# Time mixing of an RWKV-7 layer: small products of even and odd chunks laid on all four quarters of the matmul array

## The chip, the cores and the metric

The kernel runs on one core of one Trainium2 chip. The metric is the device time of one execution in microseconds. The engines are PE (TensorE: matmuls, with PEld for its weight loads), DVE (VectorE), ACT (ScalarE), POOL (GpSimd) and SP (SyncE, which issues the loads). Each takes its instructions in the order in which the program gives them; semaphores tie the engines together. A matmul contracts over partitions (rows of the array) and writes to partitions of PSUM (columns of the array). PSUM has eight banks of 2 KB for each partition; a bank holds 512 float32.

## The reference, cut to what matters

Two layers on 256 positions with 2048 features. The change touches the first, an RWKV-7 time mixing with 32 heads of 64 features:

```
def step(S, inp):
    r_t, w_t, k_t, v_t, kk_t, a_t = inp
    sa = einsum('bhvk,bhk->bhv', S, -kk_t)
    S = S * w_t[:, :, None, :] + sa[..., None] * (kk_t * a_t)[:, :, None, :] + v_t[..., None] * k_t[:, :, None, :]
    y = einsum('bhvk,bhk->bhv', S, r_t)
    return S, y
```

y is then normalised in each head, a bonus is added, and the result is gated and multiplied by `w_o`. The rest is a shared K/V, a chunked attention layer and two MLPs; they take most of the time and are not touched.

## The kernel before

**Pairs and chunks.** The recurrence is computed in four chunks of 64 positions. Two heads form a pair: their 2 x 64 features fill the 128 partitions, and there are 16 pairs. A feature-major tensor has features on partitions and positions in columns (`k`, `r`, `v`, `kr`, `bh`, `kh`). A time-major one has, for each chunk, the 64 positions on partitions: head 0's copy on partitions 0 to 63, head 1's on 64 to 127 (`vp`, `mk`, `ar`, `bk`, `da`, `co`, `u`). Nearly all of a pair's products are 64x64 or 64x128 in float32, one for each head; the head is the slice `K` of partitions on both sides. So they use two quarters of the array: rows and columns 0 to 63 for head 0, rows and columns 64 to 127 for head 1. A float32 product is two matmul instructions in the trace.

**Steps and slots.** A pair runs through 36 steps (`yield`): 8 early, 12 of inversion, 16 late. A new pair begins every 8 slots, so four or five are alive at once. In a slot each living pair issues one step (inversions first), then 1/8 of a pair's dense work: the projections `k` and `r` (`proj_steps`, 16 x 3 full matmuls each, four slots each). In three of four slots one step of an unrelated matrix-vector product follows (`ada`: a 512 KB load of `w_ada` into a `raw` buffer, then `acc` on DVE, L460). When the projections are done, 36 slots of a drain follow in which the dense work is the start of the output projection (`out_steps`). A scheduler sets each engine's order; the slots steer it.

**The steps that matter here:**

- `vp` (early step 7): `each` (L105) multiplies each chunk of `v` by `cen`; output in `ms`, copied by ACT (L186).
- First inversion step: `each` makes `bh` times `kr` for four chunks, 64x128 each, into `gr`; DVE masks it to `ar` (L217), six small ACT copies take `da` and `co` (L223, L225); POOL makes `u` and `al` from them.
- Second inversion step: two `each` with `eye` transpose two tensors into `ms`; ACT copies them to `bk` (L237).
- Further inversion steps: 32x32 products (L111) into `iv`, at the last level into `ms`; at level 2, `each` makes `kh` times `kr` into `gr`, and DVE masks it to `mk` (L267). DVE's transpose `tt` (L243) and ACT's copy `xs` lie between them.
- Late, for each chunk c three steps. First: `mk` times `vp` (L284, the value product) and `kr` times the state `zs` (L287), copied to `g`. Second: `u` times `g` (L291), negated to `sa`. Third: three products into y (L295, L298, L300) and two into the new state (L304, L306), which DVE adds to `zs` (L309, L311).

**PSUM in this stage.** `ms` two banks, `pj` two (the projections alternate), `gr`, `iv` one each, `lt` two (one for each of the two pairs that are late at once). ACT copies a finished projection out of `pj` (L870). Weights come as 512 KB loads into six `raw` buffers (L372); ACT rounds them to `wH` (L382), DVE takes the rest to `wL` (L385).

Of the kernel before, what the change touches and what calls it, by code (L numbers as in the profile page):

```python
# [77 lines left out]
class Pair:  # L78
# [23 lines left out]
    def each(self, o, lhsT, rhs):  # L102
        for c in range(4):
            for K in self.heads:
                self.b.nc.tensor.matmul(o(c)[K], lhsT(c)[K], rhs(c)[K], start=True, stop=True)  # L105
# [22 lines left out]
    def early(self):  # L128
# [55 lines left out]
        pt = b.psm().rearrange("p (a c k) -> p a c k", a=2, c=4)  # L184
        self.each(lambda c: pt[:, 0, c, :], lambda c: ch(v)[:, c, :], lambda c: cst("cen"))
        nc.scalar.copy(self.vp, pt[:, 0])  # L186
# [6 lines left out]
    def corner(self, l):  # L193
        t = self.b.psm() if l == 5 else self.b.pp.tile([P, 512], F32, tag="iv", bufs=1, name="iv")
        return t.rearrange("p (c t) -> p c t", t=H)[:, 0:4, :]

    def invert(self):
# [10 lines left out]
        ui = cst("ui").unsqueeze(1).to_broadcast([P, 4, P])  # L208
# [5 lines left out]
        pg = pp.tile([P, 4, P], F32, tag="gr", bufs=1, name="gr")  # L214
        self.each(lambda c: pg[:, c, :], lambda c: ch(bh)[:, c, :], lambda c: kr[:, c, :])
        ar = self.ar = s("ar", 3)
        nc.vector.tensor_tensor(out=ch(ar), in0=pg[:, :, C:P], in1=ui[:, :, C:P], op=ALU.mult)  # L217
# [3 lines left out]
        for i, K in enumerate(QS):  # L221
            n = H * (i % 2)
            nc.scalar.copy(da[K], pg[K, :, n:n + H])  # L223
            if i % 2 == 0:
                nc.scalar.mul(co[K], pg[K, :, H:C], -1.0)  # L225
# [7 lines left out]
        pt = b.psm().rearrange("p (a c k) -> p a c k", a=2, c=4)  # L233
        for i, t in enumerate(ts):
            self.each(lambda c: pt[:, i, c, :], lambda c: ch(t)[:, c, :], lambda c: cst("eye"))
        bk = self.bk = b.pw.tile([P, 2, 4, C], F32, tag="bk", bufs=3, name="bk")
        nc.scalar.copy(bk, pt)  # L237
# [3 lines left out]
        for l in range(1, 6):  # L241
# [21 lines left out]
            if l == 2:  # L263
                pg = pp.tile([P, 4, P], F32, tag="gr", bufs=1, name="gr")
                self.each(lambda c: pg[:, c, :], lambda c: ch(kh)[:, c, :], lambda c: kr[:, c, :])
                mk = self.mk = self.big("mk", 3)
                nc.vector.tensor_tensor(out=mk, in0=pg, in1=ui, op=ALU.mult)  # L267
            yield

    def late(self):  # L270
        b, nc, j, s, ch, v = self.b, self.b.nc, self.j, self.s, self.ch, self.v
        kr, ar, mk, bk, vp, u, pc, heads = self.kr, self.ar, self.mk, self.bk, self.vp, self.u, self.pc, self.heads
# [3 lines left out]
        pch, py = bank[:, 0, 0:3 * C].rearrange("p (a t) -> p a t", a=3), bank[:, 1, :]  # L276
        zs = None
        for c in range(4):
# [4 lines left out]
            for K in heads:  # L283
# [958 lines left out]
```

## Time and profile before

| | before |
|---|---|
| median of 3 runs | 2656.92 us (2656.05 to 2656.99) |
| span of the profiled execution | 2653.8 us |
| mean granted PE clock | 0.993 |
| PE busy | 2574.9 us, 97% |
| DVE busy | 2089.4 us, 79% |
| ACT busy | 1368.6 us, 52% |
| time mixing with pairs | about 217 to 690 us |

The page has one profiled execution. The median of the runs lies 3.1 us above its span; no time is given for that execution beside the span. A row of a timeline is: start in us, duration in us, engine, line, operation, output<-inputs, shapes, number of instructions; in square brackets the idle time of the engine just before and who ended it. Matmuls overlap in the pipeline, so the time that one takes on PE is read from one start to the next and not from its duration. Rows of a stretch give, for each of PE, PEld, DVE, ACT and POOL, the busy us and the number of instructions, then the granted clock, the DMA share and GB/s. The chain is the chain of work that ended last, followed back.

### The profile page before, as it was taken

What the parts mean: (1) busy time and instruction counts of PE and PEld (TensorE: products, weight loads), DVE (VectorE), ACT (ScalarE), POOL (GpSimd) and SP (SyncE); (2) the same over time, 40 slices, a digit from 0 to 9 for tenths busy, and PEclk for the clock granted to TensorE, in tenths of its full rate; (3) what the DMA queues carried; (4) which work ended last, traced back from release to release, by engine and by line L of the source; (5) the groups of instructions that cost most, each with busy time, mean ns of one, the idle gap of its engine ahead of it and who ended that gap; (6) DMA issues with size and microseconds to landing.
All of it is one profiled execution on the core that took longest, in us unless ns stands there. A gap on an engine that the chain in (4) does not pass through costs nothing.

```text
span 2653.8 us, 59231 instructions
## 1 busy us (share of the span) xinstructions
PE 2574.9 (97%) x24108; PEld 2257.3 (85%) x24108; DVE 2089.4 (79%) x3054; ACT 1368.6 (52%) x2484; POOL 210.6 (8%) x338
## 2 busy tenths in 40 slices
PE   7999999999999999999999999999999999999997
PEld 4788888887899888888888998887898888888886
DVE  6888878878789888888888898899887556555555
ACT  3346555555456445355365554565564464453554
POOL 1002223223110000000001000000100000000002
PEclk9999999999999999999999999999999999999999
DMA  9976656565768888989888779887766555555553
GB/s 351 320 243 220 211 181 196 180 197 196 253 234 301 325 320 320 329 325 334 325 328 293 237 247 326 313 282 263 266 216 236 191 186 188 190 187 188 189 189 121
DMA packets 207664, 663.19 MB, mean 250 GB/s; under 512 B 21408, under 2 KB 55072, under 8 KB 207392
## 3 DMA queue, kind: packets, MB, share of 16 engines
q1 hardware_dynamic: 205328, 656.89, 71.7%
q8 instruction: 189, 3.10, 0.5%
q10 hardware_dynamic: 2064, 2.53, 0.3%
q14 instruction: 83, 0.68, 0.1%
HBM read 657.23 MB, written 2.10 MB: 248 GB/s over the span
## 4 chain that ended last, share of the span: by engine, by line
PE 84%; DVE 7%; issue 4%; DMA 3%; ACT 2%; POOL 1%; SPq 0%; DVEq 0%; ACTq 0%; POOLq 0%
PE pj L416 42%; PE pj L418 21%; PE pj L405 3%; PE pj L406 3%; PE pj L407 3%; DMA raw<-w_ada 2%; DVE wL L385 2%; DVE acc L460 1%; PE iv L111 1%; PE o L405 1%; PE ms L328 1%; PE o L407 0%; ACT wH L382 0%; PE o L406 0%; PE pT L1130 0%
## 5 line engine op out<-in xcount | busy, mean ns | idle before, releaser
L385 DVE TENSOR_TENSOR wL<-raw,wH 128x1024 fp32r<-128x1024 f32 x772 | 941.1, 1220 | 342.4 <-ACT wH L382 337.2
L382 ACT CAST wH<-raw 128x1024 fp32r<-128x1024 f32 x772 | 806.0, 1045 | 762.7 <-PE pj L416 590.2
L416 PE MATMUL pj<-aHL,wH 128*128 128x512 f32 x2816 | 893.3, 398 | 1.1 <-DVE x L955 1.1
L416 PE MATMUL pj<-hHL,wH 128*128 128x512 f32 x2048 | 644.7, 396 | 0.0
L418 PEld LDWEIGHTS pj<-aHL,wL 128*128 128x128 f32 x2816 | 531.7, 189 | 123.1 <-issue 0.3
L418 PE MATMUL pj<-aHL,wL 128*128 128x256 f32 x2816 | 564.1, 281 | 0.0
L418 PEld LDWEIGHTS pj<-hHL,wL 128*128 128x128 f32 x2048 | 384.5, 188 | 91.1 <-DVE wL L385 0.9
L416 PEld LDWEIGHTS pj<-aHL,wH 128*128 128x128 f32 x2816 | 432.1, 189 | 8.6 <-issue 8.3
L418 PE MATMUL pj<-hHL,wL 128*128 128x256 f32 x2048 | 402.6, 278 | 0.4 <-DVE wL L385 0.4
L460 DVE SCALAR_TENSOR_TENSOR acc<-rada,ct,acc 128x1024 f32<-128x1024 f32 x256 | 327.3, 1278 | 7.3 <-DMA rada<-w_ada 6.9
L416 PEld LDWEIGHTS pj<-hHL,wH 128*128 128x128 f32 x2048 | 312.2, 189 | 1.3 <-DVE hHL L1001 1.1
L405 PE MATMUL pj<-aHL,wH 128*128 128x256 f32 (+1 forms) x896 | 262.5, 293 | 0.0
L406 PE MATMUL pj<-aHL,wH 128*128 128x256 f32 (+1 forms) x896 | 254.2, 284 | 0.0
L407 PE MATMUL pj<-aHL,wL 128*128 128x256 f32 (+1 forms) x896 | 253.0, 282 | 0.0
L524 POOL TENSOR_TENSOR ss<-ss,sq 128x256 f32<-128x256 f32 x56 | 51.2, 915 | 1583.7 <-ACT sq L523 1583.4
L1026 DVE SCALAR_TENSOR_TENSOR x<-pj,mod,x 128x256 f32<-128x256 f32 x256 | 123.3, 482 | 64.2 <-PE pj L418 61.2
L405 PEld LDWEIGHTS pj<-aHL,wH 128*128 128x128 f32 x896 | 169.9, 190 | 4.5 <-issue 0.2
L407 PEld LDWEIGHTS pj<-aHL,wL 128*128 128x128 f32 x896 | 170.4, 190 | 0.4 <-DVE e L851 0.2
L406 PEld LDWEIGHTS pj<-aHL,wH 128*128 128x128 f32 x896 | 169.9, 190 | 0.5
L460 DVE SCALAR_TENSOR_TENSOR acc<-raw,ct,acc 128x1024 f32<-128x1024 f32 x104 | 138.0, 1327 | 17.4 <-DMA raw<-w_ada 17.2
L998 ACT ACTIVATE t<-t 128x256 f32<-128x256 f32 x112 | 46.9, 419 | 120.2 <-DVE t L970 120.2
L1001 DVE TENSOR_TENSOR hHL<-t,hHL 128x256 fp32r<-128x256 f32 x128 | 53.9, 421 | 1.7 <-ACT t L1000 1.0
(252 smaller groups left out, 2817.6 us busy)
## 6 DMA issues: line engine op xcount, KB each, us to landing
raw<-w_up SPq DMA_DIRECT2D x256, 512.0 KB, 4.0
raw<-w_down SPq DMA_DIRECT2D x256, 512.0 KB, 3.6
rada<-w_ada SPq DMA_DIRECT2D x209, 512.0 KB, 5.5
raw<-w_ada SPq DMA_DIRECT2D x111, 512.0 KB, 4.3
rada<-w_ada_kv SPq DMA_DIRECT2D x64, 512.0 KB, 6.6
rawa<-w_ada SPq DMA_DIRECT2D x32, 512.0 KB, 6.7
rawa<-w_ada_t SPq DMA_DIRECT2D x32, 512.0 KB, 7.1
raw<-w_k SPq DMA_DIRECT2D x32, 512.0 KB, 3.6
```

The costliest lines, as they stand in the source:

```text
L382: nc.scalar.copy(Hf, raw)
L385: eng.tensor_tensor(out=Lf, in0=raw, in1=Hf, op=ALU.subtract)
L405: nc.tensor.matmul(ps, H[:, i, :], a(kt)[:, 0, :], start=(first and kt == 0), stop=False)
L406: nc.tensor.matmul(ps, H[:, i, :], a(kt)[:, 1, :], start=False, stop=False)
L407: ins = nc.tensor.matmul(ps, L[:, i, :], a(kt)[:, 0, :], start=False, stop=(last and kt == KT - 1))
L416: nc.tensor.matmul(ps, w[kt // HK][0][:, kt % HK, :], a(kt), start=(kt == 0), stop=False)
L418: ins = nc.tensor.matmul(ps[:, 0, :], w[kt // HK][1][:, kt % HK, :], a(kt)[:, 0, :], start=False, stop=(kt == KT - 1))
L460: nc.vector.scalar_tensor_tensor(out=self.acc, in0=raw, scalar=ck, in1=self.acc, op0=ALU.mult, op1=ALU.add)
L524: (eng or nc.gpsimd).tensor_tensor(out=self.ss, in0=self.ss, in1=sq, op=ALU.add)
L998: nc.scalar.activation(t, t, AF.Relu)
L1001: nc.vector.tensor_tensor(out=h[:, 1, :], in0=t, in1=h[:, 0, :], op=ALU.subtract)
L1026: nc.vector.scalar_tensor_tensor(out=x, in0=ps[:, i, :], scalar=self.mods[(layer, 5)][:, n:n + 1], in1=x, op0=ALU.mult, op1=ALU.add)
```

## The change

For odd chunks the time-major tensors lie on the other head's partitions: head 0's positions of chunks 1 and 3 on partitions 64 to 127, head 1's on 0 to 63. A product between a feature-major and a time-major tensor of an odd chunk then has its rows in one half of the array and its columns in the other, and takes the two quarters that even chunks leave free. `at(c)` gives the pairs of slices.

- `each` writes even chunks to one bank and odd chunks to another: `gr` becomes one tile of two banks (`two`). All four bursts go there, `cen` and `eye` too, which used `ms` before. The readers take a view that puts chunks back in order; they read as many elements as before.
- `pj` goes from two buffers to one to make room.
- In the late steps the value product of chunk c+1 is issued in chunk c's second step, into one of two places, and the `zs`-`kr` product of y one step earlier as well; the products of one pair share a bank as before, now under one start flag for each chunk.
- The corners of the last two pairs' inversions use `ms`, because the output projection takes `iv` two tiles earlier and both banks of `gr` afterwards; the second part of the output projection uses `lt` in place of `pj`.

```diff
+    def mm(self, o, lhsT, rhs, K, O, start, stop):
+        return self.b.nc.tensor.matmul(o[O], lhsT[K], rhs[K], start=start, stop=stop, tile_position=(K.start, O.start),
+                                       skip_group_check=True)
+    def at(self, c):
+        return tuple(zip(self.heads, self.heads[::-1] if c % 2 else self.heads))
+    def two(self):
+        return self.b.pp.tile([P, 2, 512], F32, tag="gr", bufs=1, name="gr")
-    def each(self, o, lhsT, rhs):
+    def each(self, ps, at, k, lhsT, rhs):
         for c in range(4):
-            for K in self.heads:
-                self.b.nc.tensor.matmul(o(c)[K], lhsT(c)[K], rhs(c)[K], start=True, stop=True)
+            o = at + c // 2 * k
+            for F, O in self.at(c):
+                self.mm(ps[:, c % 2, o:o + k], lhsT(c), rhs(c), F, O, True, True)
...
-        pt = b.psm().rearrange("p (a c k) -> p a c k", a=2, c=4)
-        self.each(lambda c: pt[:, 0, c, :], lambda c: ch(v)[:, c, :], lambda c: cst("cen"))
-        nc.scalar.copy(self.vp, pt[:, 0])
+        pt = self.two()
+        self.each(pt, 0, C, lambda c: ch(v)[:, c, :], lambda c: cst("cen"))
+        nc.scalar.copy(self.even_odd(self.vp), self.by_chunk(pt, 2, C))
...
-        t = self.b.psm() if l == 5 else self.b.pp.tile([P, 512], F32, tag="iv", bufs=1, name="iv")
+        t = self.b.psm() if l == 5 or self.j >= NPAIR - 2 else self.b.pp.tile([P, 512], F32, tag="iv", bufs=1, name="iv")
...
         for c in range(4):
...
-            for K in heads:
-                mm(pch[K, 0, :], mk[K, c, 0:C], vp[K, c, :], start=True, stop=(c == 0))
-            if c:
-                for K in heads:
-                    mm(pch[K, 0, :], kr[K, c, 0:C], zs[K, :], start=False, stop=True)
-            nc.scalar.copy(g, pch[:, 0, :])
+            if c == 0:
+                value(0, True)
+            else:
+                both(pgs[c % 2], kr[:, c, 0:C], zs, self.at(c), False, False)
+            nc.scalar.copy(g, pgs[c % 2])
             yield
-            for K in heads:
-                mm(pch[K, 1, :], u[K, c, :], g[K, :], start=True, stop=True)
-            nc.scalar.mul(sa, pch[:, 1, :], -1.0)
+            if c < 3:
+                value(c + 1, True)
+            if c:
+                both(y(c), zs, kr[:, c, C:P], same, c == 3, False)
+            both(pu, u[:, c, :], g, time(c), False, False)
+            nc.scalar.mul(sa, pu, -1.0)
...
-                    ps = pp.tile([P, 2 * T], F32, tag="pj", bufs=2, name="pj")[:, :T]
+                    ps = pp.tile([P, 2 * T], F32, tag="pj", bufs=1, name="pj")[:, :T]
...
-                        tag = ("pj", "pj", "gr", "iv")[n // 2]
-                        ps = pp.tile([P, 2 * T], F32, tag=tag, bufs=1 + (tag == "pj"), name="o")
-                        sums.append(ps.rearrange("p (i t) -> p i t", i=2))
+                        if n != 6:
+                            tag, k = {0: ("pj", 1), 2: ("iv", 1), 4: ("gr", 2)}[n]
+                            ps = pp.tile([P, k, 2 * T], F32, tag=tag, bufs=1, name="o")
+                            sums += [ps[:, i].rearrange("p (i t) -> p i t", i=2) for i in range(k)]
...
-                    ps = pp.tile([P, 2, T], F32, tag="pj", bufs=2, name="pj")
+                    ps = pp.tile([P, 2, T], F32, tag="lt" if begun else "pj", bufs=2, name="pj")
```

Three places in the order. In a row stand the line, the operation, output<-inputs, the output's shape, the engines whose work it waits for, and a count. L104 is the one line of `mm`, so tiles tell the products apart.

First, PE's queue in the steady part, from the older pair's inversion to the end of the `eye` burst and the late products behind it. Before:

```order
L111 MATMUL iv<-u,xs 32x32 x15
L105 MATMUL ms<-csts,s 64x64 [waits Pool_49]
L105 MATMUL ms<-csts,s 64x64 x7
L105 MATMUL ms<-csts,s 64x64 [waits Pool_49]
L105 MATMUL ms<-csts,s 64x64 x7
L295 MATMUL lt<-mk,vp 64x64 [waits Activation_49]
L295 MATMUL lt<-mk,vp 64x64
L298 MATMUL lt<-kr,zs 64x64 x2
L300 MATMUL lt<-ar,sa 64x64 x2
L304 MATMUL lt<-sa,bk 64x64 x2
L306 MATMUL lt<-vp,bk 64x64 x2
```

And the same place after:

```order
L135 MATMUL iv<-u,xs 32x32 x15
L104 MATMUL gr<-csts,s 64x64 [waits DVE_49,Activation_49,Pool_49]
L104 MATMUL gr<-csts,s 64x64 x7
L104 MATMUL gr<-csts,s 64x64 [waits Pool_49]
L104 MATMUL gr<-csts,s 64x64 x7
L104 MATMUL lt<-ar,sa 64x64 x2
L104 MATMUL lt<-mk,vp 64x64 x2
L104 MATMUL lt<-vp,bk 64x64 x2
L104 MATMUL lt<-sa,bk 64x64 x2
```

`eye` now waits for DVE and ACT, the readers of `gr`, as well; and four late products follow it where five did (`zs,kr` moved ahead).

Second, PE's queue where the projection `k` ends and `r` begins, in the steady part. Before:

```order
L111 MATMUL iv<-tt,al 32x32 x15
L295 MATMUL lt<-mk,vp 64x64 [waits Activation_49]
L295 MATMUL lt<-mk,vp 64x64
L298 MATMUL lt<-kr,zs 64x64 x2
L300 MATMUL lt<-ar,sa 64x64 x2
L304 MATMUL lt<-sa,bk 64x64 x2
L306 MATMUL lt<-vp,bk 64x64 x2
L284 MATMUL lt<-vp,mk 64x64 x2
L405 MATMUL pj<-aHL,wH 128x256
```

After:

```order
L135 MATMUL iv<-tt,al 32x32 x15
L104 MATMUL lt<-ar,sa 64x64 [waits Activation_49]
L104 MATMUL lt<-ar,sa 64x64
L104 MATMUL lt<-mk,vp 64x64 x2
L104 MATMUL lt<-vp,bk 64x64 x2
L104 MATMUL lt<-sa,bk 64x64 x2
L104 MATMUL lt<-vp,mk 64x64 x2
L437 MATMUL pj<-aHL,wH 128x256 [waits Activation_49]
```

The first matmul of `r` now waits for ACT, whose copy of `k` frees the one bank, and one late product less stands ahead of it.

Third, ACT's queue after the change at the end of the very first projection (before it is the same but for line numbers):

```order
L609 CAST aHL<-h 128x256 x15
L414 CAST wH<-raw 128x1024 [waits DMAHW4_49,DVE_49,PE_49]
L414 CAST wH<-raw 128x1024 [waits DMAHW5_49,DVE_49,PE_49]
L879 CAST bones<-csts 128x128 [waits DVE_49,Pool_49]
L902 COPY k<-pj 128x256 [waits PE_49]
```

The copy of the first `k`, for which the second projection now waits, still stands behind the casts of `aHL`, two of `wH` and one of `bones`.

65 lines of the change are left out of this document (38 added, 27 removed).

## The prediction

> **What bounds the kernel now.** I read the page first, then the busy times by stage, then the chain that ended last and the waits inside the time-mixing stage (217 to 690 us), and last the timeline of single slots.
>
> ```profile
> span 2653.8 us, 59231 instructions
> PE 2574.9 (97%) x24108; PEld 2257.3 (85%) x24108; DVE 2089.4 (79%) x3054; ACT 1368.6 (52%) x2484; POOL 210.6 (8%) x338
> ...
> 500.00:600.00 100.00, 94.79 (x2137) 85.53 (x2136) 78.00 (x146) 57.89 (x160) 25.80 (x41) 1.00 0.58 185
> ```
>
> PE is nearly always busy, and in the time-mixing stage too: 94.8 of 100 us. Taken alone that says "PE is the bound, and what it is spared comes off the end". The chain through the same stage says something else:
>
> ```profile
> by line: DMA raw<-w_ada 10.8%; issue 8.5%; DVE acc L460 7.7%; PE pj L405 5.9%; DVE wL L385 5.5%; PE iv L111 4.9%; PE pj L406 4.8%; PE pj L407 4.6%; PE ms L328 2.7%; PE gr L105 2.4%; PE ms L116 2.1%; PE ms L105 1.9%; ACT wH L382 1.8%; PE o L
> ...
> PE iv L111 <- DVE tt L243: 7.9, 12, 1.3
> ```
>
> Of the 473 us of this stage the chain runs through PE for well under half. The rest is DVE (`acc`, `wL`), the load of `w_ada` that waits for a buffer and holds up DVE, and ACT. PE and DVE take turns: PE keeps itself full and then waits for DVE's transpose. The lines that the change makes cheaper, `gr` L105 and `ms` L105, have 2.4% + 1.9% of the chain = 20.3 us. That, and not their busy time, is the first measure of what they can give.
>
> **The change, part by part.**
>
> *Products on all four quarters.* Time of one burst, from its first instruction to the next one behind it:
>
> ```profile
> 357.95 0.63 PE L105 MATMUL ms<-csts,v 64*64 64x64 f32 x16
> 358.51 0.39 PE L405 MATMUL pj<-aHL,wH 128*128 128x256 f32 x1
> ...
> 421.43 1.09 PE L105 MATMUL gr<-kr,bh 64*64 64x128 f32 x16
> 422.35 0.28 PE L291 MATMUL lt<-g,uf 64*64 64x64 f32 x4
> 425.41 1.15 PE L105 MATMUL ms<-csts,s 64*64 64x64 f32 x32
> 426.39 0.28 PE L295 MATMUL lt<-mk,vp 64*64 64x64 f32 x4
> ...
> 437.51 0.28 PE L304 MATMUL lt<-sa,bk 64*64 64x64 f32 x4
> 437.62 0.28 PE L306 MATMUL lt<-vp,bk 64*64 64x64 f32 x4
> ```
>
> A 64x64 product for both heads (four instructions) has a pitch of about 0.117 us (437.51 to 437.62 above). The `eye` burst of 32 instructions is eight of them: 0.94 of its 0.98 us. The `cen` burst of 16 is four: 0.47 of 0.56. The `gr` burst of 16 with 128 columns is four at 0.22: 0.88 of 0.92. If even and odd chunk overlap fully, half goes: 0.47 + 0.23 + 2 x 0.44 = 1.58 us for each pair, 25.3 us for 16 pairs. Lower bound 0: number and shape of instructions stay, so nothing excludes "no overlap", and a loss has no source in PE itself. I take the full overlap, because the trace has quarters at work at once where they share rows:
>
> ```profile
> 429.10 0.23 PE L111 MATMUL iv<-tt,al 32*32 32x32 f32 x3
> 429.12 0.19 PE L111 MATMUL ms<-tt,co 32*32 32x32 f32 x1
> 429.12 0.21 PE L111 MATMUL iv<-tt,al 32*32 32x32 f32 x1
> ```
>
> `ms<-tt,co` sits off the diagonal (rows 0 to 31, outputs 32 to 63, and the like), `iv<-tt,al` on it; both read the same rows, write the same partitions in different banks, and their starts interleave within 0.02 us. The change puts odd chunks into a second bank in the same way. [...]
>
> How much of 25.3 us reaches the end? On the chain lie 20.3 us of these lines, so 10.2 of the saving. Where the chain leaves PE behind such a burst, the engine that takes over was hardly waiting:
>
> ```profile
> 304.94 1.02 PE gr L105 x16
> 308.93 1.08 PE ms L105 x32
> 311.05 0.59 ACT bk L237
> ...
> 311.05 0.59 ACT L237 COPY bk<-ms 128x512 f32<-128x512 f32 x1
> ...
> 363.10 1.05 ACT L382 CAST wH<-raw 128x1024 fp32r<-128x1024 f32 x1 [0.19 <-PE pj L406]
> ```
>
> The copy of `bk` shows no idle time ahead of it, the cast at 363.10 only 0.19 us. An earlier PE end is worth no more than that idle time, unless ACT's own earlier work moves with it, which in part it does. I take 70% of 10.2: **-7.1 us**, with 0 and -25 as ends.
>
> *One bank less for the projections* (`pj` from two buffers to one; `gr` now takes two banks). Every projection's first matmul now waits for ACT's copy of the one before. At the start no pair's work lies between:
>
> ```profile
> 208.14 0.28 PE L405 MATMUL pj<-aHL,wH 128*128 128x256 f32 x1
> 210.47 0.37 ACT L870 COPY k<-pj 128x256 f32<-128x256 f32 x1
> 214.08 0.60 PE L133 MATMUL ms<-tw,lw 128*128 128x256 f32 x2
> 215.15 0.69 DVE L138 TENSOR_SCALAR s<-ms 128x512 f32<-128x512 f32 x1 [1.18 <-PE ms L134]
> ...
> 220.89 0.28 PE L405 MATMUL pj<-aHL,wH 128*128 128x256 f32 x1
> 222.26 0.36 ACT L870 COPY k<-pj 128x256 f32<-128x256 f32 x1
> 227.69 0.39 PE L116 MATMUL ms<-sq,bones 128*128 128x256 f32 x1 [1.30 <-DVE sq L125]
> ```
>
> The second projection began at 208.14; the copy ended at 210.84, behind sixteen casts of `aHL` and two of `wH` in ACT's queue, and the changed order keeps it there. So PE stands still for 2.7 us; behind it wait that projection and the pair's first product at 214.08, and DVE was idle for that product (1.18 us): nothing covers it. I take +2.5. The fourth projection (220.89 against 222.62) loses 1.7, covered by the 1.30 that PE then waits anyway: +0.7 with the smaller third switch. Ends: +2 and +5.
>
> In the steady part a pair's steps lie between:
>
> ```profile
> 436.72 1.05 ACT L382 CAST wH<-raw 128x1024 fp32r<-128x1024 f32 x1 [1.27 <-PE pj L406]
> 437.67 0.36 ACT L870 COPY k<-pj 128x256 f32<-128x256 f32 x1
> 437.95 0.39 PE L405 MATMUL pj<-aHL,wH 128*128 128x256 f32 x1
> ```
>
> The copy of k stands behind a `wH` cast and ends at 438.03; PE reached `r` at 437.95, and one late product (0.12) has moved out of this slot. PE waits 0.2 + some 0.05 for the signal, in the 13 or so full periods; behind it stand twelve projection matmuls and the next inversion step. With the chain on PE for a little under half of them that is +1.5 (ends 0 and +4). From `r` to the next `k` the burst of `gr`, `z` and now two more late products lie between: about 1 us to spare, so nothing.
>
> *`eye` and `cen` move from `ms` into `gr`.* `eye` must now wait until `ar` (DVE) and the six ACT copies of `da` and `co` have left `gr`:
>
> ```profile
> 366.97 0.26 ACT L223 COPY da<-gr 32x128 f32<-32x128 f32 x1
> 367.48 0.92 PE L105 MATMUL ms<-csts,s 64*64 64x64 f32 x24
> ...
> 336.45 0.42 DVE L217 TENSOR_TENSOR ar<-gr,csts 128x256 f32<-128x256 f32 x1
> 336.83 1.15 PE L105 MATMUL ms<-csts,s 64*64 64x64 f32 x32
> 338.10 0.26 ACT L223 COPY da<-gr 32x128 f32<-32x128 f32 x1
> 341.59 0.35 PE L111 MATMUL ms<-tt,co 32*32 32x32 f32 x10 [1.00 <-ACT bk L237]
> ```
>
> Usually the last copy ends 0.25 us ahead of `eye`; both follow `gr`, so that stays. Where DVE sits in a late `w_ada` step, `ar` comes late and `eye` would now wait 1.5 us (336.83 to 338.36). Then late products, the variance sum and twelve projection matmuls queue behind it, and ACT's `bk` waits; but PE idles 1.00 us a slot later, which takes most of it: +0.4 (0 to +4). `cen` and `gr` find their bank free by more than a microsecond. The two products of an inversion's corner no longer share `ms` with `eye`; I count nothing.
>
> *The late steps.* As many products as before; one `value` product and the `zs,kr` product of y move one step, which shifts 0.12 us between neighbouring slots and cancels over a period; odd chunks meet even ones only at seams. DMAs, their queues and POOL's work are the same in number: 0. Reads of `gr` in two banks have the same element counts: 0.
>
> *The drain.* The corners of pairs 14 and 15 use `ms`, as `iv` is given to the output projection earlier; out_proj's `lt` has the two buffers that `pj` had, so 0 there. In the order about four of these steps gain a wait on ACT; the nearest row gives half a microsecond each:
>
> ```profile
> PE ms L116 <- ACT sl L322: 1.5, 3, 0.6
> ```
>
> Half of it is taken as hidden: +1.0 (0 to +3).
>
> Sum: -7.1 + 2.5 + 0.7 + 1.5 + 0.4 + 1.0 = -1.0 us on a span of 2653.8. The median of the runs, 2656.92, lies 3.1 us above that span; the same shift gives **2655.9 us**. What a measurement here can tell from no change is about 0.2%, 5.3 us, so this is "the same".
>
> **Rivals.**
> - *PE's time counts fully* (faster). For: PE busy 94.8 of 100 us. If 60% of 25.3 us arrive, less 6.1 us of new waits, it is -9.1: 2647.8; with all of it, 2637.7. It becomes "faster" from 45% on. Against: the chain's DVE, DMA and ACT links, and the idle times of 0 and 0.19 us above. Chance 0.33.
> - *The clock is lowered more often* (slower). PE has more gaps, and after gaps its clock falls:
>
> ```profile
> 632.00:640.00 8.00, 7.98 (x127) 6.36 (x127) 5.42 (x15) 5.10 (x15) 1.54 (x3) 0.59 0.44 144
> ```
>
>   The column behind the five engines is the granted clock: 8 us ran at 0.59, a loss of 3.3 us. Two more such stretches make -1.0 + 6.6 = +5.6: 2662.5, and that is the point from which it decides. Against: in 500 to 600 the clock was 1.00 in spite of waits. [...] Chance 0.14.
> - *The quarters do not overlap* for 64x64 products, so the change doesn't do what it says: the new waits stay, +6.1: 2663.0. Against: the interleaved starts. [...] Chance 0.08.
>
> **How the numbers follow.** Forecast "about the same" 0.45 (2651.6 to 2662.2), faster 0.33, clock 0.14, no overlap 0.08; so faster 0.33, same 0.45, slower 0.22. The range goes to 2645 on the one side, where a sixth of the chance is left out, and to 2665 on the other, past both slower cases.
>
> **What would show it.** `gr`, `eye` and `cen` bursts of some 0.48, 0.51 and 0.33 us to the next instruction prove the overlap; unchanged 0.92, 0.98, 0.56 refute it. About 2.7 us between the last matmul of the first projection and the first of the second, released by ACT, prove the start's price; waits of about 0.25 us at `r`'s first matmul in the steady part the next. PE's waits for DVE's `tt` should grow from 7.9 us to some 15 to 20: there the saving goes. I am wrong on the fast side if they don't grow, on the slow side if the granted clock is below 1 in more places than now.

## The result, and the profile after

| | before | after |
|---|---|---|
| median of 5 runs each, timed in turn | 2656.05 us (2654.31 to 2656.99) | 2671.12 us (2664.64 to 2677.67) |
| span of the profiled execution | 2653.8 us | 2669.3 us |
| PE busy | 2574.9 us, 97% | 2566.0 us, 96% |

The ratio is 1.0057, interval 1.0042 to 1.0071. The changed kernel is slower by 15 us, where 1 us less had been forecast. A second job gave 1.0051 (1.0038 to 1.0064).

The top of the page after, and three rows of its busy times by stage (PE, PEld, DVE, ACT, POOL with counts, then granted clock, DMA share, GB/s):

```profile
span 2669.3 us, 59235 instructions
PE 2566.0 (96%) x24108; PEld 2244.0 (84%) x24108; DVE 2088.6 (78%) x3054; ACT 1369.4 (51%) x2484; POOL 208.3 (8%) x338
```

```profile
200.00:215.00 15.00, 12.41 (x88) 12.20 (x88) 12.41 (x26) 10.07 (x24) 0.57 (x2) 0.84 0.41 133
...
300.00:400.00 100.00, 90.67 (x2180) 81.31 (x2179) 84.94 (x153) 56.28 (x155) 24.48 (x38) 1.00 0.62 197
...
500.00:600.00 100.00, 90.86 (x2050) 80.79 (x2050) 81.20 (x153) 55.05 (x152) 24.32 (x38) 0.95 0.60 190
```

PE is less busy (90.9 of 100 us between 500 and 600; it was 94.8), and in that stage its clock, 1.00 before, is 0.95. The bursts themselves became as short as forecast. Rows of the timeline, the burst and what follows it:

```profile
427.09 0.67 PE L104 MATMUL gr<-kr,bh 64*64 64x128 f32 x16
427.58 0.28 PE L104 MATMUL lt<-vp,mk 64*64 64x64 f32 x4
...
431.83 0.69 PE L104 MATMUL gr<-csts,s 64*64 64x64 f32 x32 [0.88 <-issue]
432.35 0.28 PE L104 MATMUL lt<-ar,sa 64*64 64x64 f32 x4
```

From one start to the next: 0.49 us for `gr` (0.92 before) and 0.52 for `eye` (0.98 before). The quarters do work at once. In front of `eye` stands 0.88 us of idle time that was not there before. PE's waits from 217 to 690 us (in all, times, longest):

```profile
PE gr L104 <- issue: 10.0, 9, 2.3
PE ms L135 <- DVE tt L268: 10.0, 7, 3.8
PE iv L135 <- DVE tt L268: 6.2, 12, 1.4
PE pj L437 <- ACT k L902: 5.8, 13, 1.3
PE ms L135 <- ACT xs L277: 3.9, 1, 3.9
```

The waits for DVE's transpose `tt` have grown to 10.0 + 6.2 = 16.2 us, as the prediction said (15 to 20). Before, they were 7.9 us in front of `iv`, and 1.8 us in front of `ms`, which the prediction did not count:

```profile
PE ms L111 <- DVE tt L243: 1.8, 2, 1.2
```

So like for like 9.7 us became 16.2. New and long are the waits in front of `gr`, the thirteen waits for the copy of `k`, and one of 3.9 us at the drain's start. (For `gr` the list gives "issue", which is no engine; that these are waits for the readers of `gr` follows from the order, where `eye` waits for DVE, ACT and POOL.) The chain that ended last through the same stage has less PE in it and still the same leaders, the `w_ada` loads and DVE's `acc`:

```profile
by line: DMA raw<-w_ada 11.7%; issue 9.2%; DVE acc L492 8.6%; DVE wL L417 5.9%; PE pj L437 5.7%; PE lt L104 5.0%; PE pj L438 4.7%; PE pj L439 4.3%; ACT wH L414 3.5%; PE iv L135 2.9%; PE ms L360 2.3%; DMA raw<-w_o 2.1%; DVE sq L149 2.0%; PE 
```

The start looks as forecast, and then it does not:

```profile
208.58 0.28 PE L439 MATMUL pj<-aHL,wL 128*128 128x256 f32 x1
211.46 0.58 PE L437 MATMUL pj<-aHL,wH 128*128 128x256 f32 x1 [2.59 <-ACT k L902]
211.83 0.41 PE L438 MATMUL pj<-aHL,wH 128*128 128x256 f32 x1
212.05 0.42 PE L439 MATMUL pj<-aHL,wL 128*128 128x256 f32 x1
```

The second projection waits 2.59 us for the copy of `k` (forecast 2.7). But behind the gap its matmuls start 0.21 us apart, where 0.12 us was usual: the clock is at half from 210.8 to 217.6 us. In this profile the gap is paid, and then up to 3.4 us again for the stretch behind it. Other profiles of the same kernel have the gap without the stretch (below, e2_fill).

**The clock, counted.** The trace has a record of each stretch at which PE's clock was not full; in both profiles the granted share is 0.5 in all of them and each lasts 3.41, 6.83 or 10.24 us, but for the last one, at the program's end (12.0 us before, 13.2 after). Half of their summed length is the most that they can have cost: before 18.6 us, after 36.3 us. That difference, 17.7 us, is more than the whole loss, 15.5 us between the two spans. The mean clocks agree: (1 - 0.986) x 2669.3 = 37 us and (1 - 0.993) x 2653.8 = 19 us.

```profile
core 0: 2669.3 us, clock 0.986
```

```profile
core 0: 2653.8 us, clock 0.993
```

What stands ahead of one such stretch is seen at 549 us. First the 3.40 us ahead of it and its own first 3.40 us in the kernel after, then DVE's and PE's rows there:

```profile
548.70:552.10 3.40, 0.85 (x8) 0.64 (x6) 3.03 (x5) 2.33 (x4) 1.51 (x4) 1.00 0.55 171
552.10:555.50 3.40, 2.19 (x56) 2.04 (x57) 3.36 (x9) 3.31 (x10) 1.09 (x2) 0.50 0.82 253
```

```profile
546.84 2.16 DVE L492 SCALAR_TENSOR_TENSOR acc<-raw,ct,acc 128x1024 f32<-128x1024 f32 x1 [1.96 <-DMA raw<-w_ada]
...
549.52 1.27 DVE L492 SCALAR_TENSOR_TENSOR acc<-raw,ct,acc 128x1024 f32<-128x1024 f32 x1
550.71 0.28 DVE L283 TENSOR_TENSOR u<-u,iv 128x128 f32<-128x128 f32 x1
551.36 1.39 DVE L492 SCALAR_TENSOR_TENSOR acc<-raw,ct,acc 128x1024 f32<-128x1024 f32 x1 [0.37 <-DMA raw<-w_ada]
552.67 0.27 DVE L343 SCALAR_TENSOR_TENSOR zs<-zs,pc,lt 128x64 f32<-128x64 f32 x1
552.87 0.49 DVE L268 STREAM_TRANSPOSE tt<-u 128x128 f32<-128x128 f32 x2
553.31 0.32 PE L135 MATMUL ms<-tt,co 32*32 32x32 f32 x4 [3.76 <-DVE tt L268]
```

PE has finished its slot early and waits 3.76 us for `tt`. DVE is not idle; three `acc` steps, two of which waited for their `w_ada` load, stand ahead of `tt` in its queue. In the 3.40 us ahead PE is busy for 0.85 at a granted clock of 1.00, and from 552.1 to 558.9 us the granted clock is 0.50. Time that PE saves does not shorten this chain. PE waits longer, and here the work that then came ran at half clock. All four profiles of the changed kernel have half clock at this place; of three without the quarters (e3_noswap and its repetitions, below) one has it, so the quarters are not needed for it.

### The profile page after: what moved, and what is told of

Its sections match the earlier page's. It is cut to its first block, busy times and chain, and to the rows that moved or that the text cites. A ratio compares the mean times of both kernels' runs of the same rounds, so it can differ in the third digit from the quotient of the medians.

```text
span 2669.3 us, 59235 instructions
## 1 busy us (share of the span) xinstructions
PE 2566.0 (96%) x24108; PEld 2244.0 (84%) x24108; DVE 2088.6 (78%) x3054; ACT 1369.4 (51%) x2484; POOL 208.3 (8%) x338
## 4 chain that ended last, share of the span: by engine, by line
PE 82%; DVE 7%; ACT 3%; issue 3%; DMA 3%; POOL 1%; DVEq 0%; SPq 0%; ACTq 0%; POOLq 0%
PE pj L448 42%; PE pj L450 21%; PE pj L437 3%; PE pj L438 3%; PE pj L439 3%; DMA raw<-w_ada 2%; DVE acc L492 2%; DVE wL L417 2%; PE lt L104 1%; ACT wH L414 1%; PE o L437 1%; PE iv L135 1%; PE ms L360 0%; PE o L439 0%; PE o L438 0%
## 5 line engine op out<-in xcount | busy, mean ns | idle before, releaser
L437 PE MATMUL pj<-aHL,wH 128*128 128x256 f32 (+1 forms) x896 | 265.9, 297 | 9.0 <-ACT k L902 8.4
L438 PE MATMUL pj<-aHL,wH 128*128 128x256 f32 (+1 forms) x896 | 257.5, 287 | 0.0
L492 DVE SCALAR_TENSOR_TENSOR acc<-raw,ct,acc 128x1024 f32<-128x1024 f32 x104 | 137.4, 1322 | 21.3 <-DMA raw<-w_ada 20.8
```

Of the source, the lines that this page charges most:

```text
L437: nc.tensor.matmul(ps, H[:, i, :], a(kt)[:, 0, :], start=(first and kt == 0), stop=False)
L438: nc.tensor.matmul(ps, H[:, i, :], a(kt)[:, 1, :], start=False, stop=False)
L492: nc.vector.scalar_tensor_tensor(out=self.acc, in0=raw, scalar=ck, in1=self.acc, op0=ALU.mult, op1=ALU.add)
```

## The experiments

The theories that stood against each other: the new waits and the half clock behind them eat the gain; the late steps' new order or the drain costs it; PE's time counts after all, so that the quarters must pay somewhere. Each expectation says what its letters mean. "Lost" is half of the half-clock time of the whole span. Runs of one kernel lie within some 15 us of each other; where a difference matters it is read from the ratio to the kernel before, timed in turn on the same chip.

**e1_start.** The first two pairs' `r` projections take the bank of `iv`, which nobody uses yet.

```diff
-ps = pp.tile([P, 2 * T], F32, tag="pj", bufs=1, name="pj")[:, :T]
+spare = dst == "r" and pr.j < 2
+ps = pp.tile([P, 2 * T], F32, tag="iv" if spare else "pj", bufs=1, name="pj")[:, :T]
```

> The changed kernel, but the projections r of pairs 0 and 1 go into the bank of iv, which nobody uses yet, so the second projection doesn't wait for the copy of the first. Theory A (the loss is PE's new waits for banks, and the half clock that follows a gap): the gap of 2.6 us at 208.6 us goes, and with it the 6.8 us of half clock behind it (3.4 us lost): about 6 us less than the changed kernel, 2665 us against 2656 of before, the first bh product about 0.5 us later than before instead of 6.3. Theory B (the late steps in another order are the loss): the start is worth 2.6 us at most, and 2668 stay. Theory C (the single projection bank costs nothing after the start and the clock dips come anyway): no change, 2671.

Measured: 2663.72 us, ratio 1.0028 (1.0019 to 1.0038). Against 1.0057 and 1.0051 in the two jobs of the changed kernel, that is 6 to 8 us less, where 3.2 us of waiting had been priced. That the half-clock stretch behind the gap makes up the rest is not shown: only two of the changed kernel's four profiles have it. By the mean clock of every run (the second table under e3_noswap tells how) e1_start is 3.7 us less at full clock and loses 1.6 us less to half clock. DVE's and ACT's order also moved in this kernel, so the size is not of this place alone.

**e2_fill.** The gap stays, but 22 matmuls that nobody reads run in it.

```diff
+if dst == "r" and pr.j == 0:
+    fill = self.psm()[:, :T]
+    for i in range(22):
+        nc.tensor.matmul(fill, w[0][0][:, 0, :], xk[:, 0, 0, 0:T], start=i == 0, stop=i == 21)
```

> The changed kernel with 22 more matmuls of 256 columns, whose sums nobody reads, in the gap between the first and the second projection: PE works there and still has to wait for the bank. Theory A: the gap stays 2.6 us long, but the clock is not lowered behind it (6.8 us at half speed go): about 3.4 us less than the changed kernel, 2668, and the granted clock over 211 to 218 us is 1.00. Rival (the clock falls for another reason than an idle PE, the copy's lateness or chance): half clock stays there and the time is that of the changed kernel, 2671.

Measured: 2665.92 us, ratio 1.0038 (1.0023 to 1.0053). The timeline shows the fill and then the second projection:

```profile
210.34 2.80 PE L896 MATMUL ms<-aHL,wH 128*128 128x256 f32 x22
212.97 0.28 PE L437 MATMUL pj<-aHL,wH 128*128 128x256 f32 x1
213.09 0.28 PE L438 MATMUL pj<-aHL,wH 128*128 128x256 f32 x1
```

The same delay of 2.6 us, but the matmuls behind it start 0.12 us apart. From the first projection to the first `bh` product it takes 29.8 us, 32.7 in the profile after. That need not be the fill's doing. after_2 and after_3 leave the gap empty, have full clock behind it all the same, and take 30.0 and 29.7 us. after_3:

```profile
210.02 0.28 PE L439 MATMUL pj<-aHL,wL 128*128 128x256 f32 x1
212.52 0.38 PE L437 MATMUL pj<-aHL,wH 128*128 128x256 f32 x1 [2.22 <-ACT k L902]
212.74 0.28 PE L438 MATMUL pj<-aHL,wH 128*128 128x256 f32 x1
212.86 0.27 PE L439 MATMUL pj<-aHL,wL 128*128 128x256 f32 x1
```

Nine profiles have this gap unfilled (four of the changed kernel, three of it without the quarters, e4_pj1 and f2_corner). Seven have full clock behind it and take 29.7 to 30.0 us; after_4 has 3.4 us at half clock and takes 31.2; the first profile has 6.8 and takes 32.7. So 3.4 us at half clock cost 1.4 us here and 6.8 us cost 2.9, and whether the fill prevents it is open: chance, the rival of this expectation, gives the same rows. The ratio's interval overlaps those of the changed kernel. (On DVE and ACT the trace has the same rows in the same order as the changed kernel's, buffer numbers left out.)

**e3_noswap, noswap_2, noswap_3 and after_2, after_3, after_4.** The changed kernel with its order on every engine unaltered, but even and odd chunks on the same partitions; and the changed kernel itself again.

```diff
-return tuple(zip(self.heads, self.heads[::-1] if c % 2 else self.heads))
+return tuple(zip(self.heads, self.heads))
```

> The changed kernel without the swap: odd chunks on the same partitions as even ones, everything else (banks, views, order of the late steps) as changed. Each pair's four bursts then take their old time, 1.6 us more, 25 us in all. Theory A (PE in the slots is partly hidden): slower than the changed kernel by 8 to 20 us, 2680 to 2690; the quarters are a gain that the waits eat. Rival (the quarters give nothing to the end, the chain being elsewhere): 2671, within 4 us of the changed kernel. Rival (shorter bursts mean more gaps and more half clock, so the quarters themselves cost): faster than the changed kernel, below 2668.

> [...] In the first profile 190 us onward lost 29.5 us to half clock (half of the stretches' length), and the span without that is 2669.3 - 29.5 = 2639.9 us. Theory A (the lowered clock is what makes the changed kernel slower): the span may differ by up to 10 us, but span less half of the half-clock time stays at 2639.9 within 2 us. Rival D (the half-clock stretches only accompany other waits and cost nothing at the end): span less that time moves as far as the half-clock time does, and the span stays.

> e3_noswap a second time: the changed kernel's order on every engine, but even and odd chunks on the same partitions. First profile: span 2663.6, lost to half clock from 190 us on 15.8, difference 2647.8. Theory A: the difference is 2647.8 within 2 us again, so the swap by itself is worth 8 us at full clock, and there is less half-clock time than in the changed kernel (10 to 20 us lost against 20 to 32). Rival D: the difference moves with the half-clock time while the span stays at 2663.6.

> The changed kernel unaltered, a third profile, for the same question. Theory A: span less half of the half-clock time is 2639.9 within 2 us. Rival D: the span stays and that difference moves.

> The changed kernel unaltered, timed on the same chip and in turn with noswap_3, to settle what the quarters alone are worth. With the kernel before at 2656: 2664 to 2671 (ratio 1.003 to 1.0057).

> The changed kernel's order on every engine, even and odd chunks on the same partitions. Theory A (the PE time saved turns into waits and half clock): within 4 us of after_4. Rival C (PE's time counts, 25 us of it): 8 us or more over after_4.

Measured: e3_noswap 2667.66 us, ratio 1.0040 (1.0029 to 1.0051); in one job after_4 2669.39 us, 1.0051 (1.0038 to 1.0064), and noswap_3 2668.27 us, 1.0045 (1.0030 to 1.0061). So the quarters bring nothing that can be measured at the end: rival C, 8 us or more, falls, and so does theory A in e3_noswap's own words (2680 to 2690); 2667.66 fits both rivals there. Without the quarters the kernel is still 1.0040 and 1.0045 times the kernel before: most of the loss is not theirs. The seven profiles and two of the kernel before:

| profile | span | lost | span less lost |
|---|---|---|---|
| before, before_2 | 2653.8, 2654.1 | 18.6, 20.4 | 2635.1, 2633.7 |
| after, after_2, _3, _4 | 2669.3, 2663.9, 2664.2, 2669.8 | 36.3, 30.4, 30.3, 37.8 | 2633.0, 2633.6, 2633.9, 2632.0 |
| e3_noswap, noswap_2, _3 | 2663.6, 2673.6, 2669.7 | 22.6, 31.3, 27.6 | 2641.0, 2642.3, 2642.1 |

Spans of one program differ by up to 10 us here, and span less the lost time by 2 us at most. That speaks for theory A and against rival D (the stretches cost nothing). The expectations counted the lost time from 190 us on. Counted so the four numbers after are 2638.7 to 2642.5 and the three without the quarters 2647.8 to 2650.8, so that after_3, noswap_2 and noswap_3 miss the 2 us of theory A, by 0.6 to 1.0; the first 190 us, which the change does not touch, lose 5 to 9 us too. At full clock the quarters save 2641.8 - 2633.1 = 8.7 us (means of the rows), and they cost 33.7 - 27.2 = 6.5 us of clock.

The mean clock and the span of every timed run are on record as well, so the same can be done for all runs of all jobs. (The clock is given to three decimals, which is 1.3 us of lost time for a single run.) Means, with a standard error of some 1 us, 0.3 for the kernel before:

| kernel | runs | span | lost | span less lost |
|---|---|---|---|---|
| before | 93 | 2654.9 | 20.7 | 2634.3 |
| after; without the quarters | 13; 13 | 2667.5; 2666.7 | 31.6; 24.8 | 2635.9; 2641.9 |
| e6_eyelater; e7_eyelater_noswap | 12; 10 | 2661.7; 2663.0 | 29.5; 22.6 | 2632.2; 2640.3 |
| f1_corner and f1_again; f1_noswap | 24; 12 | 2659.6; 2658.5 | 26.8; 20.8 | 2632.8; 2637.7 |

In all three pairs the quarters save 5 to 8 us at full clock and lose 6 to 7 us to half clock. But the 2 us do not hold for all runs: span less lost differs by up to 9 us among the changed kernel's 13. Among runs of one kernel, 1 us more of lost time goes with 0.69 us more of span (230 runs of 13 kernels, standard error 0.04). So a stretch costs some two thirds of its half on average: neither all of it, as theory A has it, nor nothing, as rival D has it. Where the saving goes is seen in PE's busy time. From 217 to 690 us the first profile after and noswap_3 issue as many matmuls, in 422 and 441 us of PE's time:

```profile
217.00:690.00 473.00, 422.44 (x9600) 376.57 (x9600) 383.48 (x694) 266.28 (x722) 126.82 (x188) 0.96 0.59 191
```

```profile
217.00:690.00 473.00, 441.38 (x9594) 396.58 (x9593) 386.24 (x696) 266.84 (x722) 128.96 (x188) 0.98 0.59 192
```

All four profiles after have 422 to 425 us there, all three without the quarters 441 to 442: what PE saves, it stands idle. Busy times from 300 to 600 us, after_4 and then noswap_3:

```profile
300.00:600.00 300.00, 273.29 (x6349) 243.22 (x6347) 246.56 (x449) 169.48 (x466) 85.39 (x122) 0.98 0.60 196
```

```profile
300.00:600.00 300.00, 283.50 (x6307) 255.06 (x6307) 248.84 (x449) 170.10 (x467) 83.89 (x122) 0.99 0.60 195
```

PE's waits for `tt` in the same stretch, in the same order:

```profile
PE iv L135 <- DVE tt L268: 6.5, 11, 1.4
PE ms L135 <- DVE tt L268: 3.1, 3, 1.5
```

```profile
PE iv L135 <- DVE tt L268: 2.5, 6, 0.7
...
PE ms L135 <- DVE tt L268: 2.0, 2, 1.3
```

The quarters take 10.2 us of PE's busy time away in this stage, and 5.1 us come back as waits for `tt` alone (9.6 against 4.5); DVE's busy time is the same within 2.3 us.

**before_2.**

> The kernel before a second time. First profile: span 2653.8, lost to half clock from 190 us on 13.5, difference 2640.3. Theory A: the difference is 2640.3 within 2 us again, the same as the changed kernel's 2639.9, so that without the clock the change would be worth nothing, as predicted. Rival D: span 2653.8 whatever the half-clock time.

Measured: span 2654.1, lost 20.4, difference 2633.7 (2635.1 in the first profile). Two stretches lie elsewhere (244 and 463 us in place of 343 and 715), the difference stays within 2 us.

**e4_pj1.** The kernel before with one buffer for `pj` (the output projection's second sum gets a bank of its own, its later sums use `lt`); nothing else.

```diff
-ps = pp.tile([P, 2 * T], F32, tag="pj", bufs=2, name="pj")[:, :T]
+ps = pp.tile([P, 2 * T], F32, tag="pj", bufs=1, name="pj")[:, :T]
```

> The kernel before with one change alone: the projections have one buffer of pj instead of two (the freed bank is left for the second output sum; the output projection's second part uses lt as in the changed kernel). Theory A: the gap of 2.7 us at the start and its half clock (3.4 us), and 13 waits of 0.1 to 0.3 us later, of which half count: 2656 + 6 to 9 = 2662 to 2665. Rival (a bank less for the projections is hidden by the pairs' steps everywhere but at the start, without effect on the clock): 2658 to 2659.

Measured: 2661.93 us, ratio 1.0020 (1.0009 to 1.0031), so 5.3 us (2 to 8). Span less lost is 2638.8, 4.4 over the kernel before; the prediction's three terms for this bank are 2.5 + 0.7 + 1.5 = 4.7. The 12 timed runs give the same, 2638.7. The lost time of this profile, 24.2 us, is 4.7 above the kernel before as well (1.3 by the 12 runs), though no half clock follows this gap here: it is 2.26 us long and ends at 213.26 us, the matmuls behind its first start 0.11 to 0.12 us apart, and from 215 to 235 us the granted clock is 1.00 (0.93 in the profile after). Why half clock follows the gap in the one profile and not in the other is not shown.

**e5_eyegr.** The kernel before, `eye` alone into `gr`.

```diff
-pt = b.psm().rearrange("p (a c k) -> p a c k", a=2, c=4)
+pt = pp.tile([P, 4, P], F32, tag="gr", bufs=1, name="gr").rearrange("p a b -> p (a b)")
+pt = pt.rearrange("p (a c k) -> p a c k", a=2, c=4)
```

> The kernel before, with one edit: the eye burst writes to the single bank of gr in place of ms, so that it must wait for the readers of gr (ar on DVE, da and co on ACT), as in the changed kernel; no quarters are swapped and pj keeps two buffers. Theory A (the wait of eye for gr, about 12 us of PE idle time in the changed kernel, is a main part of the 15 us): 2 to 6 us over the kernel before, about 2659.5 to 2663, with rows of gr waiting in the list of PE's waits. Rival B (that wait is hidden, as the prediction took it at 0.4 us, and the late steps' new order or the drain makes the loss): within 1 us of the kernel before, about 2657.

Measured: 2657.16 us, ratio 1.0005 (0.9994 to 1.0016). That is 0.8 us between the medians, rival B's "within 1 us"; of theory A's 2 to 6 us the interval leaves up to 4.2. Here the waits in front of `gr` are shorter, though, than the 10.0 us at the head of the changed kernel's list:

```profile
PE gr L105 <- issue: 3.3, 6, 0.9
```

So what `eye` costs in the changed kernel, with its two-bank tile and `cen` in it too, is shown by this only in part.

**e6_eyelater and e7_eyelater_noswap.** e1_start, with `eye` and the copy of `bk` two slots later, when `gr` has long been read; and the same without the quarters.

```diff
-pt = self.two()
-for i, t in enumerate(ts):
-    self.each(pt, 2 * C * i, C, lambda c: ch(t)[:, c, :], lambda c: cst("eye"))
...
+if l == 1:
+    pt = self.two()
+    for i, t in enumerate(ts):
+        self.each(pt, 2 * C * i, C, lambda c: ch(t)[:, c, :], lambda c: cst("eye"))
```

> The changed kernel with the r projections of the first two pairs in the free bank of iv (as in e1_start, 2663.7 us), and in addition the eye burst and the copy of bk two slots later, behind the second product of inversion level 1, when gr has long been read. Theory A (eye's wait costs): some 3 to 6 us less than e1_start, 2658 to 2661, and the 9.4 us of PE's waits in front of gr shrink below 3 us. Rival B (the wait is hidden): 2663 to 2664, and as much PE idle time turns up in front of other tiles.

> The same as e6_eyelater, but even and odd chunks lie on the same partitions again, so the bursts take two quarters and some 25 us more PE time. It tells what the swap alone is worth when eye waits for nothing. Theory A (the pace between bursts is set by DVE and ACT, so the PE time saved turns into waits and half clock): within 3 us of e6_eyelater. Rival C (PE's time counts fully once the new waits are gone): 8 to 25 us over e6_eyelater.

Measured: 2663.87 us, ratio 1.0026 (1.0017 to 1.0036), no better than e1_start's 1.0028; and 2666.38 us, 1.0032 (1.0022 to 1.0042). The list of PE's waits of e6_eyelater from 217 to 690 us tells why moving `eye` brings nothing:

```profile
PE iv L135 <- DVE tt L263: 16.2, 19, 2.3
PE ms L135 <- DVE tt L263: 12.9, 11, 2.3
...
PE gr L104 <- issue: 4.3, 3, 2.4
```

In e1_start these were 9.1, 5.8 and 9.4 us. The wait has changed its place and grown: 5.1 us less in front of `gr`, 14.2 us more in front of `tt`. PE now waits for DVE's `tt` instead; but the order on DVE and ACT is another than in e1_start too. The quarters are worth nothing that can be measured again (1.0026 and 1.0032); lost time 30.1 with them, 19.5 without, span less lost 2632.4 and 2639.6.

**e8_twice.** e6_eyelater with each burst issued twice.

```diff
-        for c in range(4):
+        for c in (0, 1, 2, 3) * 2:
```

> The same as e6_eyelater with the swap, but each of the four bursts (cen, gr twice, eye) is issued twice into the same places, so PE gets back the 25 us or so that the swap saves, as work that nobody needs. Theory A (idle PE is what lowers the clock, and the bursts are not what sets the pace): within 3 us of e6_eyelater, with as few or fewer stretches at half clock. Rival C (PE's time counts fully): 8 to 25 us over e6_eyelater.

Measured: 2706.89 us, ratio 1.0192 (1.0178 to 1.0206), 43 us over e6_eyelater. That is more than theory A or rival C gave. It does not tell them apart: with the longer bursts the scheduler put DVE's, ACT's and the loads' work into another order (in the list of waits `acc` stands 42.5 us for its `w_ada` loads, 14.6 in e6_eyelater), so more than PE's time differs. Why it is 43 us is open; giving PE its time back was done cleanly only by e3_noswap, e7_eyelater_noswap and f1_noswap.

**f1_corner and f2_corner.** e1_start, and the changed kernel, with pair 14's corners of levels 1 and 2 in `iv` again. All else keeps its order, but for a few rows at this place.

```diff
-t = self.b.psm() if l == 5 or self.j >= NPAIR - 2 else ...
+t = self.b.psm() if l == 5 or self.j == NPAIR - 1 or (self.j == NPAIR - 2 and l >= 3) else ...
```

> e1_start (2663.7 us), and pair 14 keeps iv for the corners of inversion levels 1 and 2, as before the change; the output projection takes iv only later. In the changed kernel these corners wait 3.9 us for a buffer of ms, the longest single wait of PE, and 10.2 us at half clock follow it in every profile of that order. Theory A (a long wait costs itself and the half clock behind it): no wait over 2 us there, at most 3.4 us at half clock from 625 to 650 us, and 3 to 7 us less than e1_start: 2657 to 2661, about the kernel before. Rival E (the wait moves to the next tile that needs ms, or to the output projection's weights, and the clock falls there): 2662 to 2665.

> The changed kernel with the same one edit and nothing else (pair 14 keeps iv for levels 1 and 2). Theory A: 3 to 7 us less than the changed kernel, whose runs have 2664.6 to 2677.7 and a median of 2671.1 in one job and 2665.7 and 2666.0 in another: 2660 to 2666. Rival E: no difference, 2666 to 2671. Span less all time lost to half clock: 2633.5 for the changed kernel; less the wait itself that is 2630 to 2632 by theory A, 2633.5 by rival E.

Measured: 2659.66 us, ratio 1.0015 (1.0006 to 1.0025), against 1.0028 for e1_start; and 2665.52 us, 1.0035 (1.0023 to 1.0048), against 1.0057 and 1.0051. So this corner is worth 3 to 6 us, theory A's 3 to 7, though the intervals touch (f1_again, below, makes it 2 to 6). PE's waits of f2_corner from 630 to 650 us:

```profile
PE ms L140 <- ACT xs L277: 2.0, 1, 2.0
PE gr L104 <- issue: 0.9, 1, 0.9
PE iv L135 <- DVE tt L268: 0.8, 1, 0.8
```

Half of the 3.9 us is still waited at the next tile of `ms` (2.7 us in f1_corner), as rival E had it. The single profiles do not show the half clock that theory A puts behind this wait: from 625 to 650 us it is 10.2 us in two profiles of the changed kernel and 3.4 in the other two (not 10.2 in every one, as the expectation says), 3.4 in f2_corner, 10.2 in e1_start and 6.8 in f1_corner, where 3.4 at most was expected, and 6.8 in both profiles of the kernel before. Span less lost is 2640.7 in f2_corner, which misses both theories; it is 2635.1 in f1_corner and 2627.6 in e1_start. These are single profiles, up to 8 us from what the tables above would give. The timed runs are steadier: f1_corner's kernel loses 3.2 us less to half clock than e1_start (26.8 against 30.0), f2_corner 5.8 us less than the changed kernel (25.8 against 31.6), with nothing gained at full clock.

**f1_again and f1_noswap.** Both long waits gone, with and without the quarters, in one job.

> f1_corner once more (both long new waits taken away, quarters on), for the comparison with f1_noswap on one chip: 2658 to 2661.

> f1_corner with even and odd chunks on the same partitions, order on every engine unaltered. Theory A: within 4 us of f1_again, with less half-clock time. Rival C (without the two long waits the quarters pay): 8 us or more over f1_again, 2667 or above. The quarters' share taken in the prediction, 7.1 us, lies between and would show as 2665 to 2667.

Measured: 2662.16 us, ratio 1.0019 (1.0007 to 1.0031), and 2659.88 us, 1.0017 (1.0009 to 1.0026). The first is above the 2658 to 2661 that was expected, 2.5 us over f1_corner, the same kernel. The quarters gain nothing here either; the prediction's 7.1 us would have shown as 2665 to 2667 in f1_noswap. Lost time 27.5 us with them, 17.6 without; span less lost 2633.2 and 2639.7. The mean clocks, f1_again and then f1_noswap:

```profile
core 0: 2660.7 us, clock 0.990
```

```profile
core 0: 2657.3 us, clock 0.993
```

No version came out ahead of the kernel before; f1_corner and its repetition are 1.5 to 8 us over it.

## Why the prediction was wrong, point by point

- **The step that failed** is the term for the quarters, -7.1, and with it the clock, which the sum leaves out: it stood only as a rival ("two more such stretches", 6.6 us) with a chance of 0.14. At the end the quarters are worth nothing that can be measured: with them the changed kernel's runs are 0.8 us longer than without (13 runs each, standard error 1.4). The other terms add up to +6.1, but without the quarters the changed kernel is 11.8 us over the kernel before; of that e4_pj1 shows 5.3 for the bank, f1_corner, f1_again and f2_corner 2 to 6 for one corner of the drain, and e5_eyegr about 1 for `eye`.
- **The sum at full clock** comes out nearly right. By the table of all runs, span less lost is 1.7 us more after than before, by the profiles 1.3 us less (2633.1 against 2634.4), where -1.0 was worked out; the lost time grew by 10.9 us, by the profiles by 14.2 (19.5 to 33.7). That this agrees so well is partly luck: single profiles of other kernels were off by up to 8 us, and a stretch costs about two thirds of its half. At that price the clock explains some 7.5 of the 12.6 us between the mean spans. No run changes the clock alone, so its share is worked out and not shown by an experiment.
- **Quarters, -7.1.** The bursts are as forecast (0.49 and 0.52 us; `cen` 0.43, with a late product among its instructions, against 0.33), and 5 to 8 us are saved at full clock in three pairs of kernels of equal order. But PE stands idle for the time it saves, and 6 to 7 us of clock go with it. The prediction's own argument, that an earlier end of PE is worth no more than the idle time of the engine that takes over, was right: with the 0 and 0.19 us that it found there the term would have been near 0, and 70% was taken all the same.
- **The start, +2.5 and +0.7.** The wait was right (2.59 us, released by the copy of `k`). Left out was the half clock behind it: 2.9 us in the first profile after, 1.4 in the fourth, none in the other two.
- **`r` behind the copy of `k`, +1.5.** Thirteen waits as forecast, 5.8 us in all. The ten of the steady part, from 328.9 us on, take 0.16 to 0.41 us, 0.23 on average, where 0.25 was forecast (the 0.05 in it for the signal is what the trace has: a copy ends at 328.87 us, the matmul starts at 328.92); the first three, at 229.0, 250.6 and 273.9 us, take 3.5 together. With the two terms of the start the bank's price is 4.7; e4_pj1 measured 5.3 (2 to 8).
- **`eye`, +0.4.** Nothing speaks against it: e5_eyegr measured +1.3 us by its ratio, with zero in its interval and 4.2 as its upper end. That PE's idle time in front of `gr` would else have been spent a slot later fits e6_eyelater, but is not shown alone.
- **The drain, +1.0.** Mis-sized. One step, pair 14's corner, waits 3.9 us alone, eight times the half microsecond taken, and is worth 2 to 6 us.
- **The late steps, 0.** No run has them alone. f1_noswap, which has them together with `eye`, the rest of the drain and the steady waits at `r`, is 3.6 us over the kernel before (mean spans), so they cannot be much.
- **Rivals.** PE's time counts fully: refuted in three pairs. The quarters do not overlap: refuted by the bursts. The sign for the slow side, "if the granted clock is below 1 in more places than now", is what happened: from 190 to 800 us there are seven to ten such places in the four profiles after, four in each of the two before. The gaps ahead of that rival's row at 632 us are two waits of PE, 1.25 us up to 629.56 and 1.32 us up to 631.96.

## What to carry to other kernels

Before crediting PE time that a change saves, ask who is late next: where DVE or a load sets the pace, a faster PE only waits. Here 10.2 us less of PE's busy time from 300 to 600 us brought 5.1 us more of waits for `tt`, and ahead of each of the ten stretches at half clock from 190 to 800 us in the profile after, PE was busy for only 0.83 to 2.04 of 3.41 us. Price a new wait on PE at its own length plus what half clock may follow: behind the gap of 2.5 us at the start that was 0 in seven profiles of nine, 1.4 and 2.9 us in the others. Check how the clock stands in each stage, not only its mean. Compare programs whose order on every engine is the same, and take several profiles of each: the time lost to the clock differed by up to 8.7 us between profiles of one program (22.6 and 31.3 without the quarters).

## What the runs showed of the hardware that was not expected

- Ahead of no stretch at half clock from 190 to 800 us was PE idle for the whole 3.41 us, neither in the first profile before nor in the first after: it was busy for 1.31 to 2.09 us of them ahead of the four before, and for 0.83 to 2.04 us ahead of the ten after. Its busy time does not tell by itself whether half clock follows: from 541.22 to 544.63 us before it was busy for 1.89 us, from 302.96 to 306.37 us after for 2.06 us, and the granted clock of the next 3.40 us was 1.00 both times.
- The same program has its stretches at half clock at other places in another profile: two of them at 343 and 715 us in the first profile before, at 244 and 463 us in before_2. Among runs of one kernel, 1 us more of lost time goes with 0.69 us more of span.
- The same program with the same gap of 2.5 us in PE's work can have half clock behind the gap or not. The stretch from before the gap to a later product took 29.7 to 30.0 us without it, 31.2 with 3.4 us of it and 32.7 with 6.8 us.
